# Experts sorted by load: twelve places of 128 slots and twenty of 64, with high and low token parts side by side

## The chip, the core and the metric

The kernel is one launch on one core of a Trainium2 chip. TensorE (PE) multiplies matrices, and its weight loads are a row of their own (PEld); VectorE (DVE), ScalarE (ACT) and GpSimd (POOL) compute elementwise, SyncE (SP) issues most of the DMAs. Each engine takes its own instructions in the order in which they stand. Tensors lie in device memory and pass through SBUF, which has 128 partitions; TensorE adds up in PSUM. The metric is the device time of one execution, in microseconds (us); lower is better.

## The reference

Two transformer blocks on 1024 tokens of width 1024: a mixer with attention and a gated delta rule, then a mixture of experts; a second block with a long convolution (hyena) and a gated feed-forward part. The change lies in the mixture of experts of the first block. Each token picks one of 4 groups and in it 2 of 8 experts, so 2048 pairs of token and gate go to 32 experts:

```python
hid = jax.nn.silu(xblk @ w1[e]) * (xblk @ w3[e])      # w1, w3: 1024 x 512
return hid @ w2[e]                                    # w2: 512 x 1024
...
yb = lax.map(run, (xb, blk_expert)).reshape(cap, D) * buf_w[:, None].astype(t.dtype)
y = jnp.zeros((N, D), t.dtype).at[buf_tok].add(yb)
```

Everything is float32, with sums that are near float32's accuracy.

## The kernel before

**Split products.** TensorE multiplies a shortened format here (fp32r), so every operand is split into hi, its rounding, and lo, the rest. `mm3` (L229 to L233) makes a product of three matmuls: hi(x) hi(w), hi(x) lo(w), lo(x) hi(w). The tokens stand as the stationary operand of 128 columns, one column a slot; the weights move, 512 columns at a time.

**Weights.** Each expert has 6 MB, which come in six pieces of 1 MB: w1 and w3 in two halves each of K (kg), then w2 in two. `weights` (L212 to L227) has SyncE load a piece into raw (L218), ScalarE cast it to hi in two halves of 1024 columns (L223), and VectorE subtract lo = raw - hi in two halves (L226). The pieces of w1 and w3 have four rows of 2 KB in a partition, those of w2 two of 4 KB. There are five raw buffers and three pairs of hi and lo (`wpool "We",5,3`), so a cast waits until TensorE has read the third piece before it, and a load waits for lo of the fifth piece before it.

**A block** (`block` in `moe`) is one expert's work on 128 slots: GpSimd gathers the token rows (L1410, into one of three xg); eight transposes (L1417) put them into PSUM, ScalarE casts xh (L1419), VectorE subtracts xl (L1420); 48 matmuls make h1 and h3 in two PSUM banks (mm); silu on ScalarE (L1432), mul on VectorE (L1433) give hs; four transposes (L1436), sh (L1439), sl (L1440); 24 matmuls with w2 into two banks (acc); VectorE scales by gate and a row (yo, L1455, two of 512 columns); GpSimd adds the rows into d_x in memory (L1456).

**Order of the experts.** `route` counts the tokens of each expert on the chip. The first place is expert 0. Of the others, the three first that have more than 128 tokens get a second gather of 128 slots in their own block (NTWO = 3, at TWO_AT), which shares the pieces. What is over goes to a loop at the end whose count is read from memory (`more`); here it ran no pass. So there are 32 + 3 = 35 gathers and 32 x 6 = 192 pieces.

**Beside it** runs the spectrum: a generator for the filter of the second block, whose matmuls (sp, L327, L354, L362), VectorE operations (L332 to L365) and stores (L367) a scheduler spreads over the blocks. At the end of the routing, val (L1355, L1356) holds for each slot column the token and gate, L1360 multiplies them into columns, and tokI (L1366) is what the gathers read. Behind the stage `hyena` begins with a norm that loads x back (L1501).

Of the kernel before, what the change touches and what calls it, by code (L numbers as in the profile page):

```python
# [8 lines left out]
F32 = mybir.dt.float32  # L9
# [6 lines left out]
P = 128  # L16
S = 1024
D = 1024
EPS = 1e-6
NEXP = 32  # L20
NTWO = 3
TWO_AT = (8, 14, 20)
NBLK = 48
# [6 lines left out]
def shape_constants():  # L30
# [52 lines left out]
    io[:, 156:163] = P * np.arange(1, 8)[None, :]  # L83
# [30 lines left out]
class Builder:  # L114
    def __init__(self, tc, ins, ctx):
        self.tc, self.nc, self.i, self.ctx = tc, tc.nc, ins, ctx
        self.right = 0
        self.cst = ctx.enter_context(tc.tile_pool(name="cst", bufs=1))
# [93 lines left out]
    def weights(self, src, a, b, eng=None, pieces=False):  # L212
# [7 lines left out]
        n = a * b  # L220
# [694 lines left out]
    def attention(self, cx, qn, kn, vv, oaT):  # L915
# [14 lines left out]
        for h in range(4):  # L930
# [84 lines left out]
            self.rsqrt(nrm[5], nrm[3], 65536.0, EPS, "a")  # L1015
# [191 lines left out]
    def route(self, pool, lg):  # L1207

# [94 lines left out]
        V.tensor_sub(ch, two[:, 1:33], two[:, 0:32])
        V.scalar_tensor_tensor(ch1, two[:, 0:32], 1.0, ch, op0=ALU.add, op1=ALU.mult)

        pos, cd = T("pos", 32), T("cd", 32)
        V.tensor_scalar(pos, two[:, 0:32], -1.0, two[:, 32:33], op0=ALU.mult, op1=ALU.add)
        V.tensor_add(pos, pos, io[:, 0:32])
        V.scalar_tensor_tensor(cd, two[:, 0:32], 1.0, pos, op0=ALU.add, op1=ALU.subtract)
        V.tensor_mul(cd, cd, ch)  # L1310
        V.tensor_add(pos, pos, cd)
        V.memset(pos[:, 0:1], 0.0)

        V.tensor_sub(pk, obs[:, 0:32], ch)
        V.tensor_scalar(pk, pk, 1.0, 32.0, op0=ALU.add, op1=ALU.mult)
        V.tensor_add(pk, pk, pos)
        V.scalar_tensor_tensor(pk, ch1, 1024.0, pk, op0=ALU.mult, op1=ALU.add)

        blk, slot = T("blk", 2, 8), T("slot", 2, 8)
        big, q, sel = T("big", 16, 7), T("q", 16), T("sel", 8, 32)  # L1320
        rk, pa = T("rk", 2, 8), T("pa", 2, 8)
        for u in range(2):
            for src, dst in ((R, rk), (pk[:, None, :].to_broadcast([P, 8, 32]), pa)):
                V.tensor_mul(sel, E[u], src)
                V.tensor_reduce(dst[:, u, :], sel, axis=AX.X, op=ALU.add)
        rkf, paf = (x.rearrange("p a b -> p (a b)") for x in (rk, pa))
        blkf, slotf = (x.rearrange("p a b -> p (a b)") for x in (blk, slot))
        V.tensor_tensor(big, rkf[:, :, None].to_broadcast([P, 16, 7]), io[:, None, 156:163].to_broadcast([P, 16, 7]), op=ALU.is_ge)
        V.tensor_reduce(q, big, axis=AX.X, op=ALU.add)
        V.scalar_tensor_tensor(slotf, q, -float(P), rkf, op0=ALU.mult, op1=ALU.add)  # L1330
        pi, ei, oi, ci = (T(n, 16, dt=I32) for n in ("pi", "ei", "oi", "ci"))
        V.tensor_copy(pi, paf)
        V.tensor_scalar(ei, pi, 31, None, op0=ALU.bitwise_and)
        V.tensor_scalar(oi, pi, 5, 31, op0=ALU.logical_shift_right, op1=ALU.bitwise_and)
        V.tensor_scalar(ci, pi, 10, None, op0=ALU.logical_shift_right)

        sec, far, is2 = T("sec", 16), T("far", 16), T("is2", 16)
        V.scalar_tensor_tensor(sec, q, 1.0, ci, op0=ALU.is_equal, op1=ALU.mult)
        V.tensor_scalar(is2, sec, 0.5, None, op0=ALU.is_gt)
        V.scalar_tensor_tensor(far, q, float(NTWO + 30), oi, op0=ALU.add, op1=ALU.add)  # L1340
        V.scalar_tensor_tensor(sec, sec, 31.0, far, op0=ALU.add, op1=ALU.subtract)
        V.tensor_mul(sec, sec, is2)
        V.tensor_add(far, far, sec)
        V.tensor_sub(far, far, ei)
# [530 lines left out]
```

## Time and profile before

| | before |
|---|---|
| median of three runs | 3263.32 us (3260.86 to 3264.44) |
| the profiled execution | 3262.82 us, its span 3261.0 us |
| TensorE matmuls busy | 3098.0 us, 95% |
| TensorE weight loads | 2524.8 us, 77% |
| VectorE | 2440.2 us, 75% |
| ScalarE | 1318.7 us, 40% |
| the experts' stage | from about 1267 to 2000 us |

A busy time is the sum of the durations of an engine's instructions; an engine at 95% can still wait for a few moments in every step. A duration is longer than the step to the next instruction where instructions overlap, so a series is costed by the distance of the starts. The weight-load row shows how long the loading of stationary operands takes, beside the matmuls. In a row of waits the name in front waits for the name behind the arrow.

### The profile page before, as it was taken

To read this page: it belongs to the slowest core of one execution; us is meant where nothing else is said; L and a number is where in the kernel's file an instruction comes from. 1 tells how busy PE (TensorE), PEld (TensorE's weight loads), DVE (VectorE), ACT (ScalarE), POOL (GpSimd) and SP (SyncE) were. 2 spreads that over 40 slices of the span, in tenths; PEclk is the share of its full clock that TensorE was granted. 3 is DMA by queue.
4 is the path that set the end of the run, shared out by engine and by line. 5 is a ranking of instruction groups with operands and counts; after the bars stand their busy time and mean duration, and the time that the engine had idled before them with its cause. 6 is when DMAs were issued, how large, how long until landed. Compare 5 with 4: busy or idle time off the path is not lost.

```text
span 3261.0 us, 42410 instructions
## 1 busy us (share of the span) xinstructions
PE 3098.0 (95%) x15667; PEld 2524.8 (77%) x15667; DVE 2440.2 (75%) x4596; ACT 1318.7 (40%) x2158; POOL 170.8 (5%) x155
## 2 busy tenths in 40 slices
PE   5999999999999977999999997999999999999998
PEld 4778999877777855777777775888878788888886
DVE  7888878757766668887788886777789765755767
ACT  3443333345553214665676664423233221211222
POOL 0001000000000012111121110000000000000000
PEclk9999999999999977999999998999999999999999
DMA  5554332344236544998988996311224221111111
GB/s 193 191 186 129 98 111 87 115 135 144 83 123 231 191 152 150 323 338 276 331 279 273 331 350 208 112 65 65 78 103 172 83 63 44 48 52 52 46 39 71
DMA packets 323789, 499.25 MB, mean 153 GB/s; under 512 B 24586, under 2 KB 179382, under 8 KB 322557
## 3 DMA queue, kind: packets, MB, share of 16 engines
q1 hardware_dynamic: 305693, 465.03, 41.9%
q0 software_dynamic: 10080, 16.81, 2.3%
q10 hardware_dynamic: 7808, 14.68, 1.3%
q8 instruction: 124, 2.03, 0.3%
q14 instruction: 84, 0.69, 0.1%
HBM read 437.95 MB, written 78.41 MB: 158 GB/s over the span
## 4 chain that ended last, share of the span: by engine, by line
PE 54%; DVE 7%; DMA 1%; issue 1%; ACT 1%; DVEq 0%; ACTq 0%; POOLq 0%; SPq 0%
PE mm L239 7%; PE mm L242 7%; PE mm L240 7%; PE mm L231 4%; PE mm L233 3%; PE mm L232 3%; PE acc L233 2%; PE acc L231 2%; PE acc L232 2%; PE sp L362 1%; PE acc L239 1%; PE acc L240 1%; PE acc L242 1%; PE tp L242 1%; PE tp L240 1%; PE tp L239 1%
## 5 line engine op out<-in xcount | busy, mean ns | idle before, releaser
L226 DVE TENSOR_TENSOR lo<-raw,hi 128x1024 fp32r<-128x1024 f32 x464 | 551.1, 1225 | 144.8 <-ACT hi L223 144.3
L223 ACT CAST hi<-raw 128x1024 fp32r<-128x1024 f32 x468 | 471.9, 1049 | 260.6 <-PE acc L233 128.0
L240 PE MATMUL mm<-y_hi,lo 128*128 128x512 f32 x1072 | 419.8, 392 | 0.0
L239 PE MATMUL mm<-y_lo,hi 128*128 128x512 f32 x1072 | 418.9, 391 | 0.0
L242 PE MATMUL mm<-y_hi,hi 128*128 128x512 f32 x1072 | 269.3, 391 | 0.0
L240 PEld LDWEIGHTS mm<-y_hi,lo 128*128 128x128 f32 x1072 | 201.3, 188 | 41.1
L239 PEld LDWEIGHTS mm<-y_lo,hi 128*128 128x128 f32 x1072 | 201.4, 188 | 40.9
L242 PEld LDWEIGHTS mm<-y_hi,hi 128*128 128x128 f32 x1072 | 200.8, 188 | 40.8
L1791 DVE SCALAR_TENSOR_TENSOR cv<-gpad,fcw,cv 128x1024 f32<-128x1024 f32 x176 | 225.9, 1283 | 5.1
L231 PE MATMUL mm<-hi,xh 128*128 128x512 f32 x512 | 202.6, 396 | 0.0
L232 PE MATMUL mm<-lo,xh 128*128 128x512 f32 x512 | 200.7, 392 | 0.2 <-DVE lo L226 0.2
L233 PE MATMUL mm<-hi,xl 128*128 128x512 f32 x512 | 200.7, 393 | 0.0
L239 PE MATMUL mm<-h_lo,hi 128*128 128x512 f32 x448 | 179.1, 400 | 1.0 <-DVE h_lo L210 1.0
L240 PE MATMUL mm<-h_hi,lo 128*128 128x512 f32 x448 | 178.1, 398 | 0.0
L412 DVE SCALAR_TENSOR_TENSOR ada<-araw,c,ada 128x512 f32<-128x512 f32 (+1 forms) x176 | 139.9, 795 | 27.0 <-DMA araw<-in_w_ada 14.2
L239 PE MATMUL mm<-lo,h_hi 128*128 128x256 f32 x512 | 135.5, 295 | 0.1
L240 PE MATMUL mm<-hi,h_lo 128*128 128x256 f32 x512 | 132.8, 290 | 0.0
L242 PE MATMUL mm<-h_hi,hi 128*128 128x512 f32 x448 | 122.8, 400 | 0.0
L231 PEld LDWEIGHTS mm<-hi,xh 128*128 128x128 f32 x512 | 96.5, 189 | 23.4 <-ACT xh L1419 2.3
L233 PEld LDWEIGHTS mm<-hi,xl 128*128 128x128 f32 x512 | 96.6, 189 | 21.5 <-DVE xl L1420 1.3
L1735 ACT CAST hi<-raw 128x2048 fp32r<-128x2048 f32 (+2 forms) x36 | 63.7, 1770 | 119.8 <-PE tp L242 104.1
L232 PEld LDWEIGHTS mm<-lo,xh 128*128 128x128 f32 x512 | 96.6, 189 | 19.9 <-DVE lo L226 0.6
(605 smaller groups left out, 6762.6 us busy)
## 6 DMA issues: line engine op xcount, KB each, us to landing
raw<-in_w SPq DMA_DIRECT2D x192, 1024.0 KB
araw<-in_mod_w SPq DMA_DIRECT2D x96, 256.0 KB
raw<-in_w_in SPq DMA_DIRECT2D x22, 1024.0 KB
raw<-in_ffn_w_up SPq DMA_DIRECT2D x44, 512.0 KB
araw<-in_w_ada SPq DMA_DIRECT2D x64, 256.0 KB
raw<-in_hy_w_in SPq DMA_DIRECT2D x12, 1024.0 KB
araw<-in_w_ada SPq DMA_DIRECT2D x16, 512.0 KB
d_G<-cy ACTq DMA_DIRECT2D x16, 512.0 KB
```

Of the source, the lines that this page charges most:

```text
L223: nc.scalar.copy(fh[:, qs], fr[:, qs])
L226: (eng or nc.vector).tensor_tensor(fl[:, qs], fr[:, qs], fh[:, qs].bitcast(F32), op=ALU.subtract)
L231: nc.tensor.matmul(out, lhs[0], rhs[0], start=start, stop=False)
L232: nc.tensor.matmul(out, lhs[0], rhs[1], start=False, stop=False)
L233: nc.tensor.matmul(out, lhs[1], rhs[0], start=False, stop=stop)
L239: nc.tensor.matmul(out, a[0], b[1], start=start and k == 0, stop=False)
L240: nc.tensor.matmul(out, a[1], b[0], start=False, stop=False)
L242: nc.tensor.matmul(out, a[0], b[0], start=False, stop=stop and k == n - 1)
L362: nc.tensor.matmul(a, fo[:, j, n, :], sd[4 + j][u], start=j == 0, stop=j == 3)
L412: V.scalar_tensor_tensor(acc, raw, c[:, k:k + 1], acc, op0=ALU.mult, op1=ALU.add)
L1735: nc.scalar.copy(hi, raw)
L1791: nc.vector.scalar_tensor_tensor(c3, g[:, di:di + 16, dj:dj + 64], col(k), c3, op0=ALU.mult, op1=ALU.add)
```

## The change

The experts are sorted by load on the chip into places. Twelve places are large (128 slots): expert 0, and the heaviest as found by the counts; places 1 to 3 have 64 slots more in a second gather, for experts with more than 128 tokens. Twenty are small, with 64 slots, and one gather of 128 rows fetches the tokens of two of them. In a small block the stationary operand holds 64 hi and 64 lo columns side by side, so a k tile needs two matmuls (with lo(w), with hi(w)) rather than three; the two halves of the rows in PSUM are added afterwards (L1470 copies rows 64 to 127 down, L1471 adds). w2 keeps three matmuls, with 64 columns as the stationary operand. The second slots of the three large places are made like small blocks. The order is the first place, then eleven large places, each of the first ten followed by a pair of small ones.

w1 and w3 come as two rows of 4 KB in a partition, and the transposes take the token columns with step 2 to match. Cast and lo of a piece are one instruction of 2048 columns each (`whole`). `route` computes two scans together (over 128, over 64) and a third for what is over, has 57 slot columns rather than 48, and copies the lower half of ten columns to the first partitions (tokB, gateB). A scratch name in a norm and the constants' pool change too.

```diff
-NTWO = 3
-TWO_AT = (8, 14, 20)
-NBLK = 48
+NTWO = 3
+NLARGE = 12
+C1 = NLARGE
+C2 = C1 + (NEXP - NLARGE) // 2
+C3 = C2 + NTWO
+NBLK = C3 + 32
...
-        for q in range(2):
-            qs = slice(q * n // 2, (q + 1) * n // 2)
+        m = 1 if whole else 2
+        parts = [slice(q * a * b // m, (q + 1) * a * b // m) for q in range(m)]
+        for qs in parts:
             nc.scalar.copy(fh[:, qs], fr[:, qs])
-        for q in range(2):
-            qs = slice(q * n // 2, (q + 1) * n // 2)
+        for qs in parts:
             (eng or nc.vector).tensor_tensor(fl[:, qs], fr[:, qs], fh[:, qs].bitcast(F32), op=ALU.subtract)
...
+                m = n // 64 if small else 1
+                x = wk.tile([P, 8, m, 2, n // m], F32R, name="x")
+                for kg in range(2):
+                    t = self.tp((P, 4, n))
+                    for q in range(4):
+                        nc.tensor.transpose(t[:, q, :], xg[0:n, bass.ds(kg * 512 + q // 2 * 256 + q % 2, P, step=2)], self.ident[0:n, 0:n])
+                    ks = slice(4 * kg, 4 * kg + 4)
+                    tt = t.rearrange("p q (m n) -> p q m n", m=m)
+                    nc.scalar.copy(x[:, ks, :, 0, :], tt)
+                    nc.vector.tensor_sub(x[:, ks, :, 1, :], tt, x[:, ks, :, 0, :].bitcast(F32))
...
-                        wt = self.weights(w("w3" if u else "w1")[kg * 512:kg * 512 + 512, :].rearrange("(k p) n -> p k n", p=P), 4, 512, eng if kg == 0 else None)
+                        src = w("w3" if u else "w1")[kg * 512:kg * 512 + 512, :].rearrange("(a p b) n -> p a (b n)", p=P, b=2)
+                        wt = [x.rearrange("p a (b n) -> p (a b) n", b=2) for x in self.weights(src, 2, 1024, eng if kg == 0 else None, True)]
...
+                                    xx = x[:, kk].rearrange("p l n -> p (l n)")
+                                    nc.tensor.matmul(h[n][u], xx, wt[1][:, k, :], start=kk == 0, stop=False)
+                                    nc.tensor.matmul(h[n][u], xx, wt[0][:, k, :], start=False, stop=kk == 7)
...
+                        v = wk.tile([P, 512], F32, name="hs", bufs=3)
+                        for o, a in zip((s, v), h[n]):
+                            nc.scalar.copy(o[0:64], a[64:P])
+                            nc.vector.tensor_add(o[0:64], a[0:64], o[0:64])
+                        nc.scalar.activation(s[0:64], s[0:64], AF.Silu)
+                        nc.vector.tensor_mul(s[0:64], s[0:64], v[0:64])
...
+            for n, b in enumerate(rest):
+                block(place(b), large(b))
+                if n < C2 - C1:
+                    small(C1 + n)
```

What stands in a row, in the names of the program: a number behind a name is one buffer's tile, mm and acc are PSUM banks, hi, lo, raw a piece of the weights.

VectorE, before, one plain block from lo of its first w2 piece to yo (ab and sd are the spectrum's, xl the next block's tokens):

```order
L226 TENSOR_TENSOR lo_16325<-raw_16326,hi_16324 128x1024 x2
L341 TENSOR_TENSOR ab_18864<-ab_18864,sd31_18862 128x512
L332 TENSOR_TENSOR sd40_18873<-sp_18871,win_18869 128x512
L1433 TENSOR_TENSOR hs_16310<-hs_16310,mm_16229 128x512
L226 TENSOR_TENSOR lo_16345<-raw_16346,hi_16344 128x1024 x2
L1440 TENSOR_TENSOR sl_16319<-tp_16313,sh_16318 128x512
L1420 TENSOR_TENSOR xl_16383<-tp_16384,xh_16382 128x512
L226 TENSOR_TENSOR lo_16401<-raw_16402,hi_16400 128x1024 x2
L332 TENSOR_TENSOR sd41_18877<-sp_18875,win_18869 128x512
L226 TENSOR_TENSOR lo_16421<-raw_16422,hi_16420 128x1024
L1455 SCALAR_TENSOR_TENSOR yo_16364<-acc_16322,gateS_12691,g2row_12731 128x512
L1455 SCALAR_TENSOR_TENSOR yo_16364<-acc_16323,gateS_12691,g2row_12731 128x512
```

VectorE, after, one small block over the same part; L1471 are the two adds, L1473 the mul, L1480 sl, L1496 yo:

```order
L230 TENSOR_TENSOR lo_17363<-raw_17364,hi_17362 128x2048
L1471 TENSOR_TENSOR hs_17343<-mm_17285,hs_17343 64x512
L1471 TENSOR_TENSOR hs_17344<-mm_17286,hs_17344 64x512
L230 TENSOR_TENSOR lo_17381<-raw_17382,hi_17380 128x2048
L1473 TENSOR_TENSOR hs_17343<-hs_17343,hs_17344 64x512
L230 TENSOR_TENSOR lo_17416<-raw_17417,hi_17415 128x2048
L1480 TENSOR_TENSOR sl_17357<-tp_17351,sh_17356 128x256
L230 TENSOR_TENSOR lo_17430<-raw_17431,hi_17429 128x2048
L1496 SCALAR_TENSOR_TENSOR yo_17398<-acc_17360,gateS_12705,g2row_12749 64x512
L1496 SCALAR_TENSOR_TENSOR yo_17398<-acc_17361,gateS_12705,g2row_12749 64x512
L230 TENSOR_TENSOR lo_17444<-raw_17445,hi_17443 128x2048
```

Two adds and a whole lo now stand between the last w3 piece and mul, and another whole lo between mul and sl.

ScalarE, before, a plain block from the cast of its first w2 piece to sh:

```order
L223 CAST hi_17117<-raw_17119 128x1024 x2
L1432 ACTIVATE hs_17103<-mm_17021 128x512
L223 CAST hi_17137<-raw_17139 128x1024 x2
L223 CAST hi_17193<-raw_17195 128x1024 x2
L1439 CAST sh_17111<-tp_17106 128x512
```

ScalarE, after, a small block over the same part, up to the cast that waits for the first w2 piece's buffer:

```order
L228 CAST hi_17362<-raw_17364 128x2048
L1470 COPY hs_17343<-mm_17285 64x512
L228 CAST hi_17380<-raw_17382 128x2048
L1470 COPY hs_17344<-mm_17286 64x512
L228 CAST hi_17415<-raw_17417 128x2048
L1472 ACTIVATE hs_17343<-hs_17343 64x512
L1479 CAST sh_17356<-tp_17351 128x256
L228 CAST hi_17429<-raw_17431 128x2048
```

Each copy of a half-sum has a whole cast ahead of it, and silu stands behind a third.

TensorE, before, between the last matmuls with w3 and the first with w2:

```order
L232 MATMUL mm_17192<-lo_17254,xh_17175 128x512
L233 MATMUL mm_17192<-hi_17253,xl_17176 128x512
L362 MATMUL sp_18946<-sd60_18903,dftl_18801 128x512
L362 MATMUL sp_18946<-sd70_18918,dftl_18801 128x512
L362 MATMUL sp_18956<-sd40_18873,dftl_18801 128x512
L1436 MATMUL tp_17276<-ident_66,hs_17273 128x128 x4
L1417 MATMUL tp_17347<-ident_66,xg1_12726 128x128 x4
L362 MATMUL sp_18956<-sd50_18888,dftl_18801 128x512
L231 MATMUL acc_17285<-hi_17287,sh_17281 128x512
L232 MATMUL acc_17285<-lo_17288,sh_17281 128x512
L233 MATMUL acc_17285<-hi_17287,sl_17282 128x512
```

TensorE, after, in a small block at the same place:

```order
L1460 MATMUL mm_17286<-hi_17329,x_17261 128x512
L1459 MATMUL mm_17286<-lo_17330,x_17261 128x512
L1460 MATMUL mm_17286<-hi_17329,x_17261 128x512
L1476 MATMUL tp_17351<-ident_66,hs_17343 128x64 x4
L235 MATMUL acc_17360<-hi_17362,sh_17356 64x512
L236 MATMUL acc_17360<-lo_17363,sh_17356 64x512
L235 MATMUL acc_17361<-hi_17362,sh_17356 64x512
L236 MATMUL acc_17361<-lo_17363,sh_17356 64x512
L237 MATMUL acc_17360<-hi_17362,sl_17357 64x512
L237 MATMUL acc_17361<-hi_17362,sl_17357 64x512
```

The spectrum's matmuls that stood around the transposes of hs (sp) are gone from here: after, the last of them stands in the block of the 22nd expert, before, behind the last block. sl is needed by the fifth matmul rather than the third. On VectorE, ahead of val in the routing, 11 of the spectrum's operations (sd, ab, asum) stand before and 20 after.

## Rows read from the trace of the kernel before

**Rows 1.** Busy time per engine on the page: us, share of span, instructions.

```profile
PE 3098.0 (95%) x15667; PEld 2524.8 (77%) x15667; DVE 2440.2 (75%) x4596; ACT 1318.7 (40%) x2158; POOL 170.8 (5%) x155
```

**Rows 2.** Stretches: length, engines' busy us (instructions), TensorE clock, DMA share, GB/s.

```profile
1862.20:1883.60 21.40, 21.40 (x93) 16.18 (x92) 18.68 (x21) 14.64 (x17) 2.64 (x2) 1.00 0.98 348
...
1462.00:1492.60 30.60, 30.60 (x137) 24.58 (x136) 17.47 (x19) 12.52 (x15) 1.45 (x2) 1.00 0.70 241
1492.60:1522.50 29.90, 29.90 (x131) 22.40 (x130) 24.43 (x28) 17.33 (x21) 7.91 (x5) 1.00 0.82 258
1301.00:1990.00 689.00, 685.62 (x2985) 523.60 (x2986) 584.48 (x632) 457.64 (x530) 101.70 (x71) 1.00 0.90 311
```

**Rows 3.** Timeline of TensorE inside w2: start us, length, instruction.

```profile
1868.39 0.39 PE L232 MATMUL acc<-lo,sh 128*128 128x512 f32 x1
1868.62 0.39 PE L233 MATMUL acc<-hi,sl 128*128 128x512 f32 x1
```

**Rows 4.** Line L1436, transposes of hs: ns min/median/max, first and last start.

```profile
L1436 PE MATMUL tp<-ident,hs x140: 270/273/332, 1280.7 to 1993.6; 128*128 128x128 f32 x140
```

**Rows 5.** Timeline of VectorE in that plain block; brackets: idle before, releaser.

```profile
1863.52 0.68 DVE L1433 TENSOR_TENSOR hs<-hs,mm 128x512 f32<-128x512 f32 x1
1864.12 2.35 DVE L226 TENSOR_TENSOR lo<-raw,hi 128x1024 fp32r<-128x1024 f32 x2
...
1870.81 1.23 DVE L226 TENSOR_TENSOR lo<-raw,hi 128x1024 fp32r<-128x1024 f32 x1 [1.95 <-ACT hi L223]
...
1875.01 6.89 DVE L226 TENSOR_TENSOR lo<-raw,hi 128x1024 fp32r<-128x1024 f32 x6
```

**Rows 6.** Timeline of ScalarE in the same block.

```profile
1869.73 2.00 ACT L223 CAST hi<-raw 128x1024 fp32r<-128x1024 f32 x2 [2.42 <-PE acc L233]
```

**Rows 7.** Groups of the stage, 1250 to 2050: busy us, mean ns, idle before.

```profile
L1455 DVE SCALAR_TENSOR_TENSOR yo<-acc,gateS,g2row 128x512 f32<-128x512 f32 x64 | 45.1, 744 | 7.4 <-PE acc L233 7.4
...
L1410 POOL DMA_INDIRECT xg<-d_h,tokI x35 | 38.0, 1085 | 373.6 <-PE tp L1417 363.5 <-DMA raw<-in_w 9.0 <-issue 0.9
```

**Rows 8.** Groups of a later stage (2450 to 3230) with whole 2048-column pieces.

```profile
L1735 ACT CAST hi<-raw 128x2048 fp32r<-128x2048 f32 x28 | 53.6, 1914 | 113.5 <-PE tp L242 104.1 <-DMA raw<-in_ffn_w_up 9.1 <-PE acc L242 0.2
...
L210 DVE TENSOR_TENSOR lo<-raw,hi 128x2048 fp32r<-128x2048 f32 x28 | 64.0, 2287 | 11.8 <-ACT hi L1735 11.6
```

**Rows 9.** Groups of other stages with 64 partitions or 256 columns.

```profile
L955 ACT CAST kT<-tp 64x512 fp32r<-64x512 f32 x16 | 9.3, 583 | 0.3
...
L956 DVE CAST kT<-tp 64x512 fp32r<-64x512 f32 x16 | 10.7, 682 | 6.7 <-ACT kT L955 6.6
...
L849 DVE TENSOR_TENSOR gXt<-gXt,acc 128x256 f32<-128x256 f32 x96 | 39.9, 418 | 15.2 <-PE acc L792 14.0
```

**Rows 10.** Waits, 1250 to 2020: total us, times, longest.

```profile
ACT hi L223 <- PE acc L233: 128.0, 59, 5.3
...
ACT hi L223 <- DMA raw<-in_w: 3.4, 3, 1.8
...
SPq L218 <- DVE lo L226: 537.5, 183, 9.0
```

**Rows 11.** Four stretches around an idle time of TensorE, in an earlier stage.

```profile
1018.00:1021.40 3.40, 3.40 (x16) 2.63 (x14) 1.82 (x2) 1.05 (x1) 0.00 (x0) 1.00 1.00 315
1021.40:1024.60 3.20, 0.18 (x2) 0.03 (x1) 1.96 (x3) 2.09 (x2) 0.00 (x0) 1.00 1.04 379
1024.60:1028.00 3.40, 3.40 (x8) 2.45 (x9) 2.40 (x2) 1.04 (x1) 0.00 (x0) 0.52 0.86 273
1028.00:1032.00 4.00, 3.41 (x15) 2.43 (x15) 1.22 (x1) 1.05 (x1) 0.00 (x0) 0.98 0.87 343
```

**Rows 12.** Timelines of TensorE and VectorE at the end of routing.

```profile
1244.20 6.58 PE L1360 MATMUL acc<-r_val,r_ls 128*128 128x96 f32 x32 [0.66 <-DVE r_val L1356]
...
1251.77 3.07 DVE L1366 CAST tokI<-r_row 128x48 int32<-128x48 f32 x1
```

**Rows 13.** Timeline of ScalarE behind the stage.

```profile
2014.40 1.04 ACT L223 CAST hi<-raw 128x1024 fp32r<-128x1024 f32 x1 [19.00 <-DMA d_spec<-so]
```

More of the change, by code (lines that the diff above doesn't have):

```diff
@@ L210, in lo, with weights @@
         self.nc.vector.tensor_sub(out, src, hi.bitcast(F32))
-    def weights(self, src, a, b, eng=None, pieces=False):
+    def weights(self, src, a, b, eng=None, whole=False):
         nc = self.nc
@@ L1322, in route @@
-        for u in range(2):
[L1323 to L1344, printed above, removed]
-        V.scalar_tensor_tensor(far, q, 0.5, far, op0=ALU.is_gt, op1=ALU.mult)
@@ L1346, in route @@
-        V.tensor_add(blkf, far, ei)
+        for k, lim in ((0, 128.0), (1, 64.0)):
+            V.tensor_scalar(ob[0][:, k, 2:33], cnt[:, 1:32], lim, None, op0=ALU.is_gt)
+        run = sums(ob)
+        s2, s1, n2, n1 = run[:, 0, 0:32], run[:, 1, 0:32], run[:, 0, 32:33], run[:, 1, 32:33]
+        pos, p1, d1, d2 = T("pos", 32), T("p1", 32), T("d1", 32), T("d2", 32)
+        V.tensor_scalar(pos, s1, -1.0, n1, op0=ALU.mult, op1=ALU.add)
+        V.tensor_add(pos, pos, io[:, 0:32])
+        V.tensor_sub(p1, s1, s2)
@@ new lines, in route @@
+        V.tensor_scalar(p1, p1, n2, 1.0, op0=ALU.add, op1=ALU.add)
+        V.tensor_sub(d1, p1, pos)
+        V.scalar_tensor_tensor(d1, cnt, 64.0, d1, op0=ALU.is_gt, op1=ALU.mult)
+        V.scalar_tensor_tensor(d2, s2, 1.0, p1, op0=ALU.add, op1=ALU.subtract)
+        V.scalar_tensor_tensor(d2, cnt, 128.0, d2, op0=ALU.is_gt, op1=ALU.mult)
+        V.tensor_add(pos, pos, d1)
+        V.tensor_add(pos, pos, d2)
+        V.memset(pos[:, 0:1], 0.0)
+        cap, two, beg, mov, far = (T(n, 32) for n in ("cap", "two", "beg", "mov", "far"))
@@ new lines, in route @@
+        V.tensor_reduce(nb, gtm, axis=AX.X, op=ALU.add)
+        oc = [T("oc0", 1, 33), T("oc1", 1, 33)]
+        for x in oc:
+            V.memset(x, 0.0)
+        V.tensor_copy(oc[0][:, 0, 1:33], nb)
+        obs = sums(oc)[:, 0]
+        V.tensor_scalar(beg, pos, float(NLARGE), None, op0=ALU.min)
+        V.tensor_add(beg, beg, pos)
+        V.tensor_scalar(beg, beg, 64.0, None, op0=ALU.mult)
+        V.tensor_scalar(mov, two, 2.0 * (C2 - 2), None, op0=ALU.mult)
+        V.scalar_tensor_tensor(far, obs[:, 0:32], 128.0, beg, op0=ALU.mult, op1=ALU.subtract)
@@ L1441, in block @@
                     hs.append((sh, sl))
[L1442 removed]
+                y = [[(self.mm if n < len(slots) - 1 else self.acc)() for _ in range(2)] for n in N]
                 for kg in range(2):
[L1444 to L1445 removed]
+                    wt = self.weights(w("w2")[kg * 256:kg * 256 + 256, :].rearrange("(k p) n -> p k n", p=P), 2, 1024, None, True)
+                    for n, (sh, sl) in zip(N, hs):
+                        rows = slots[n][0]
                         for k in range(2):
@@ L1470, in moe, with place, large @@
-            for b in order:
-                reg = nc.sync.value_load(self.order[0:1, b - 1:b], min_val=0, max_val=31)
-                block(of(reg), [col(b)] + ([col(31 + b)] if b <= NTWO else []))
+            def place(b):
+                return of(nc.sync.value_load(self.order[0:1, b - 1:b], min_val=0, max_val=31))
+            def large(b):
+                tg = lambda c, n: (self.tokI[0:n, c:c + 1], self.gateS[0:n, c:c + 1])
+                t, g = tg(b, P)
+                slots = [(P, gather(t), t, g)]
+                if 0 < b <= NTWO:
+                    t, g = tg(C2 + b - 1, 64)
+                    slots.append((64, gather(t, 64, True)[:, :, 0], t, g))
+                return slots
@@ new lines, in small @@
+            def small(c):
+                x = gather(self.tokI[:, c:c + 1], P, True)
+                for e, (t, g) in enumerate(((self.tokI[0:64, c:c + 1], self.gateS[0:64, c:c + 1]),
+                                            (self.tokB[:, c - C1:c - C1 + 1], self.gateB[:, c - C1:c - C1 + 1]))):
+                    block(place(NLARGE + 2 * (c - C1) + e), [(64, x[:, :, e], t, g)])
+            block(lambda nm: I[nm][0, 0], large(0), nc.gpsimd)
+            rest = list(range(NTWO + 1, NLARGE))
```

163 lines of the change are left out of this document (81 added, 82 removed).

## The prediction

> **What bounds the kernel now.** I read the page first: TensorE shows 95% of the span busy [rows 1], so the question is whether that holds in the stage that changes. The table of stretches answers it [rows 2]. One plain block, 1862.2 to 1883.6, takes 21.40 us, and TensorE is busy for all of it, VectorE for 18.68, ScalarE for 14.64. A block with a second gather takes 30.60 + 29.90 = 60.5 us with the plain block behind it, so the second slots cost 39.1 - 21.4 = 17.7 us; DMA is at 0.70 there and VectorE at 17.47 of 30.6: that one is bound by TensorE. From 1301 to 1990 TensorE is busy 685.6 of 689 us at the full clock. The transposes of hs start at 1280.7 and 1993.6 first and last [rows 4]: 31 intervals in 713 us, close to 31 x 21.4 + 3 x 17.7 = 716.5.
>
> So TensorE ends last, but the others stand close behind. VectorE has 2.7 us of slack in a plain block, no more. The waits [rows 10] show a ring: ScalarE's hi cast waits 128.0 us in 59 waits for the second matmuls (acc), because only three hi/lo buffers exist; VectorE's lo waits for that cast; SyncE waits 537.5 us for lo to give raw back. The casts waited for their DMA only 3.4 us in all, three times, so transfers end first. What must be asked of a shorter TensorE part is how far the ring VectorE, cast, buffer lets it through.
>
> **TensorE's work falls.** One 512-column matmul follows the other by 0.23 us [rows 3]. Before, each of the 35 gathers has 48 + 24 = 72 of them, some 16.5 us, and 12 transposes, about 1 us (one is 0.27 [rows 4], overlapping the next): 17.6, with the spectrum's matmuls filling up to 21.4. After, 12 large blocks keep that; 20 small blocks and three second parts have 32 + 24 = 56, or 13.4 us. That is 23 x 4.2 = 97 us less TensorE work. It is the most that this edit can bring.
>
> **VectorE's work does not fall.** A weight piece of 2048 columns costs it one subtraction rather than two: 2.29 us alone [rows 8], 2.20 back to back if it overlaps its neighbour as a 512-wide one does (0.68, but 0.60 to the next [rows 5]); before, 6.89 for six halves, 2.30 a piece [rows 5]. Six pieces: 13.2, against 13.8. A small block adds two additions of 64x512 for the halves; 64 partitions are no cheaper than 128 (0.682 [rows 9]), so 1.2. Mul is 0.6, sl 0.36 (0.418 [rows 9]), the two yo 1.33 (0.744 each [rows 7], less the overlap). Per small block 13.2 + 1.2 + 0.6 + 0.36 + 1.33 = 16.7 us, plus half of a shared xl. So even a perfect small block is no shorter than about 17 us.
>
> **The small block, step by step.** VectorE's new order is lo(w2a), two adds, lo(w2b), mul, lo(next w1a), sl, lo(next w3a), two yo, and two more lo. Call 0 the end of lo for the last w3 piece. Its 8 matmuls end at about 2.0. VectorE does lo(w2a) to 2.2; ScalarE copies the second half-sum 2.1 to 2.7 (0.583 [rows 9]); the adds end at 3.4; lo(w2b) at 5.6; silu on ScalarE stands behind a cast of 1.914 [rows 8] and is done by 5.2; mul ends at 6.2. Before, the last matmul led to silu and mul at once; now a copy, an add and a whole 2.2 us lo lie between, and TensorE has nothing from 2.0 to 6.2. Then come transposes to about 7.0, the sh cast to 7.5 (shorter than that copy), and four matmuls to 8.4. VectorE meanwhile does lo(next w1a) to 8.4 and sl to 8.8; only then do the other eight w2a matmuls run, to 10.7. The next w3a piece needs the hi/lo buffer that w2a holds, so its cast runs 10.75 to 12.7 and lo starts there: a hole of about 4 us on VectorE. Before, the same place had a hole of 1.95, with half casts of 1 us (2.00 for two) [rows 5, 6]; the whole cast lengthens it. The sum is 16.8 + 4.0 = 20.85 us against 21.4. **The small block is then no longer bound by TensorE, and it gains half a microsecond, not four.** Bounds: 17 with no hole, 22.5 where spectrum work stands in the queue.
>
> **Large blocks.** After a small pair comes a large block. Its xl (two at 0.6) stands on VectorE behind the yo, at 16.3 to 17.5 on the clock above, and its third product waits for it; from there its four pieces need 4 x 12 x 0.227 = 10.9 us of TensorE. From last w3 matmul to last w3 matmul that is 24.4 to 25.3, say 24.9. From large to first small it is 20 to 21.8, say 20.5, as the large block's own chain has silu and mul without copies. A triple is 24.9 + 20.5 + 20.85 = 66.25, against 3 x 21.4 = 64.3. Ten triples: **+19.5** (by the ends of the legs +9 to +41; lower only if the hole closes, which is R1).
>
> **Second slots.** Three of them, at 56 matmuls and 0.7 us of transposes rather than 72: 12.5 us rather than 17.7, as TensorE bounds there. **-15.6** (0 to -17).
>
> **Spectrum work on VectorE** (0.6 us an operation [rows 5]) was covered by the 2.7 us of slack. In small blocks there is none outside the hole. In the order, five small blocks carry two or three such operations outside it, 13 in all: **+8** (0 to +15).
>
> **Clock.** Where TensorE had run 0.18 us in a stretch of 3.20, the stretch of 3.40 us after it was granted 0.52, the lower level of 1.2 GHz, and ran 8 matmuls where 16 ran in 3.40 us before [rows 11]. A small block has TensorE waiting about 4.2 us before its transposes. Eight matmuls at the low level cost 3.4 - 8 x 0.227 = 1.6 us more; part falls while sl is awaited. I take 0.8 for each of 20: **+16** (0 to +35). The Trainium skill ("TensorE: Matmul & The Clock Gate", HAM oscillation — how this bites in real kernels) says that kernels with few rows that wait between groups of matmuls fall to the low clock every time and lose by it. It agrees with the row; its rule is R2 below.
>
> **Routing.** Two scans rather than one, about 3.5 us of small operations on a VectorE that was nearly full; 20 rather than 11 spectrum operations now stand ahead of val, 9 x 0.6 = 5.4; L1360's 32 matmuls of 96 columns (6.58 us [rows 12]) get 114, some 0.5. Part of that lies beside the transfers of the first weights, and the work that moved ahead leaves the first block 2 us shorter. tokI, at 1251.77 [rows 12], comes later by **+7** (0 to +11).
>
> **Tail.** TensorE's spectrum work now ends with ten experts to go; before it went on behind the last block and a hi cast waited 19.00 us for the spectrum's store, until 2014.40 [rows 13]. The loads of x need the scatter (SyncE waited 11.4 us for it), which stays: **-3** (0 to -8).
>
> **4 KB rows** are a DMA matter. The ring gives raw back too late for DMA to matter [rows 10], so nothing, unless the interval falls below about 18 us. The step-2 transposes, the renamed scratch and the constants' pool: nothing.
>
> **Sum.** 19.5 - 15.6 + 8 + 16 + 7 - 3 = +31.9 us. The profiled execution took 3262.82, half a microsecond under the median of 3263.32, so about 3295.
>
> **Rivals.** *R1, faster.* The relief gets through: VectorE's hole closes, as casts and w2a matmuls slip under other work. TensorE at 100% in every stretch [rows 2] speaks for it; VectorE's 17 us floor and the three buffers speak against. If small blocks came at 17 to 18, 20 x 3.7 = 74 us go, with the second slots 90, less 7 for routing: 3262.8 - 90 + 7 - 3 = 3177. Halfway, at 19.5 us and large blocks at 22, 20 x 1.9 - 10 x 0.6 + 15.6 - 4 gives about 3219. The other terms leave 8 + 16 + 7 - 3 - 15.6 = 12.4 us to be earned by ten triples, so it decides at a triple of 63.1 us: small blocks at 20.5 with 22 for the large leg, or 19.5 with 24. The Trainium skill ("Perfetto Trace Analysis", Identifying the Most-Contended Engine) holds that busy matmuls overstate TensorE and its weight loads should be read instead. By that rule TensorE has slack already, 16.18 of 21.40 being 76%, and taking work off it is worth less; it speaks against R1 and this change.
>
> *R2, slower still.* The low clock lasts on: in each small block all 24 w2 matmuls and the next piece's run at 0.43 rather than 0.23 us (1.6 us for every eight). With 2 to 3 us more on the path in 20 blocks, 40 to 60: 3335 to 3355. Against it, the row after the low one is back at 0.98 [rows 11].
>
> *R3, the change does not do what it says.* If more than eleven of experts 1 to 31 carry over 64 tokens, or over three carry more than 128, the closing loop runs; every pass is a serial block of at least 21 us. Before, the 35 gathers [rows 7] are 32 + 3, so nothing overflowed there, but the new capacities are other ones; two overflows give 3340.
>
> **How the numbers follow.** Forecast 0.58, its own range 3265 to 3325; R1 0.27; R2 0.12; R3 0.03. A measurement of this kernel tells 0.2%, about 6.5 us, from no change. Slower: 0.47 of the forecast + 0.15 of R2 and R3 = 0.62. Same: 0.08 + 0.04 of R1 = 0.12. Faster: 0.03 + 0.23 = 0.26. The range reaches down into half of R1 and up to the start of R2: 3205 to 3330.
>
> **What would show it.** Right: transposes of hs 20 to 22 us apart in small pairs, 24 to 25 before a large block; ScalarE's hi cast waiting for acc in every small block, and a VectorE gap of about 4 us behind sl; TensorE clearly under full in the stage, with stretches granted less than 1.00; VectorE above 80%. Wrong: small intervals under 19 us (R1), or clock under 0.8 over the stage (R2), or more than 35 large and small gathers (R3: 12 + 10 + 3 = 25 are due). tokI more than 11 us later, or not at all later, would make the routing term wrong.

## The result, and the profile after

The changed kernel takes 3361.31 us in the median (3357.9 to 3365.47) against 3263.78: 1.030 times as long, interval 1.028 to 1.032. The forecast was slower, and slower it is, but by 97 us and not by 32; the time lies above the range. The profiled execution has a span of 3356.1 us, 95.1 more than before.

The page's busy shares, to be read beside [rows 1]:

```profile
PE 3077.4 (92%) x15219; PEld 2438.3 (73%) x15219; DVE 2438.7 (73%) x4447; ACT 1305.6 (39%) x1990; POOL 237.0 (7%) x143
```

The transposes of hs, to be read beside [rows 4]:

```profile
L1476 PE MATMUL tp<-ident,hs x140: 216/273/472, 1286.7 to 2075.8; 64*128 64x64 f32 x92, 128*128 128x128 f32 x48
```

This row cuts the 95 us into three. The first transposes start 6.0 us later than the 1280.7 of [rows 4]; the 31 intervals take 789.1 us and not 712.9, which is 76.2; and what lies behind the last block takes 12.9 us longer (3356.1 - 2075.8 = 1280.3, before 1267.4), though none of its code changed.

A late small block, one without spectrum work, on VectorE (start, length, instruction, idle before and releaser):

```profile
1966.83 6.68 DVE L230 TENSOR_TENSOR lo<-raw,hi 128x2048 fp32r<-128x2048 f32 x3
1973.43 1.48 DVE L1471 TENSOR_TENSOR hs<-mm,hs 64x512 f32<-64x512 f32 x2
1974.83 2.27 DVE L230 TENSOR_TENSOR lo<-raw,hi 128x2048 fp32r<-128x2048 f32 x1
1977.03 0.68 DVE L1473 TENSOR_TENSOR hs<-hs 64x512 f32<-64x512 f32 x1
1977.63 2.28 DVE L230 TENSOR_TENSOR lo<-raw,hi 128x2048 fp32r<-128x2048 f32 x1
1979.84 0.41 DVE L1480 TENSOR_TENSOR sl<-tp,sh 128x256 fp32r<-128x256 f32 x1
1985.02 2.29 DVE L230 TENSOR_TENSOR lo<-raw,hi 128x2048 fp32r<-128x2048 f32 x1 [4.78 <-ACT hi L228]
```

and on TensorE:

```profile
1973.10 0.40 PE L1460 MATMUL mm<-hi,x 128*128 128x512 f32 x1
1977.77 0.64 PE L1476 MATMUL tp<-ident,hs 64*128 64x64 f32 x4 [4.27 <-DVE hs L1473]
```

and in stretches (length, busy us of TensorE, weight loads, VectorE, ScalarE and GpSimd, granted clock, DMA share, GB/s), the second just behind that wait and the third the whole block:

```profile
1977.80:1981.40 3.60, 3.60 (x13) 2.41 (x14) 2.45 (x2) 0.37 (x1) 0.00 (x0) 0.53 1.04 336
1966.30:1989.00 22.70, 15.04 (x62) 9.84 (x61) 17.80 (x14) 13.77 (x12) 7.71 (x2) 0.92 0.82 291
```

This is the block of the prediction: adds, a whole lo, mul, a whole lo, sl, then a hole. TensorE waits 4.27 us for mul where 4.2 was said, and runs at a granted 0.53 behind it. It came out at 22.7 us, not at 20.85 and 0.8: the hole behind sl is 4.78 us rather than 4, and VectorE is busy for 17.80 us of the stretch rather than 16.8. But such blocks are the good ones. The scheduler puts other work into others, and in four of the 23 small parts (20 blocks and three second parts) it puts two whole lo between the second add and mul; there TensorE waits 5.9 to 6.7 us. One of the four:

```profile
1587.20 4.47 DVE L230 TENSOR_TENSOR lo<-raw,hi 128x2048 fp32r<-128x2048 f32 x2
1591.60 0.68 DVE L1473 TENSOR_TENSOR hs<-hs 64x512 f32<-64x512 f32 x1
```

### The profile page after: what moved, and what is told of

Read it like the earlier page. It is cut to its first block, busy times and chain, and to the rows that moved or that the text cites. A ratio compares the mean times of both kernels' runs of the same rounds, so it can differ in the third digit from the quotient of the medians.

```text
span 3356.1 us, 41235 instructions
## 1 busy us (share of the span) xinstructions
PE 3077.4 (92%) x15219; PEld 2438.3 (73%) x15219; DVE 2438.7 (73%) x4447; ACT 1305.6 (39%) x1990; POOL 237.0 (7%) x143
## 5 line engine op out<-in xcount | busy, mean ns | idle before, releaser
L230 DVE TENSOR_TENSOR lo<-raw,hi 128x2048 fp32r<-128x2048 f32 (+1 forms) x274 | 531.7, 1957 | 220.0 <-ACT hi L228 216.7
L228 ACT CAST hi<-raw 128x2048 fp32r<-128x2048 f32 (+1 forms) x276 | 449.6, 1644 | 270.3 <-PE acc L237 144.5
L1459 PE MATMUL mm<-lo,x 128*128 128x512 f32 x320 | 137.5, 430 | 26.7 <-DVE lo L230 22.3
L1460 PE MATMUL mm<-hi,x 128*128 128x512 f32 x320 | 128.0, 400 | 0.0
L1497 POOL DMA_INDIRECT d_x<-yo,tokI x25 | 96.5, 3859 | 345.4 <-DVE yo L1496 311.5
L235 PE MATMUL acc<-hi,sh 128*64 128x512 f32 (+1 forms) x256 | 117.2, 458 | 3.5 <-ACT sh L1479 3.5
L236 PE MATMUL acc<-lo,sh 128*64 128x512 f32 (+1 forms) x256 | 111.4, 435 | 0.0
L1848 DVE TENSOR_SCALAR cv<-gpad,fcw,fcb 128x1024 f32<-128x1024 f32 x22 | 17.9, 814 | 121.7 <-ACT gpad L1842 121.6
```

What stands on the lines that cost most here:

```text
L235: nc.tensor.matmul(out, lhs[0], rhs[0], start=start, stop=False)
L236: nc.tensor.matmul(out, lhs[0], rhs[1], start=False, stop=False)
L1459: nc.tensor.matmul(h[n][u], xx, wt[1][:, k, :], start=kk == 0, stop=False)
L1460: nc.tensor.matmul(h[n][u], xx, wt[0][:, k, :], start=False, stop=kk == 7)
L1497: nc.gpsimd.indirect_dma_start(out=self.x1, out_offset=bass.IndirectOffsetOnAxis(ap=tcol, axis=0), in_=yo[0:rows], in_offset=None, bounds_ ...
```

## The experiments

**Where is the loss behind the stage?** The feed-forward part has the same code in both kernels and TensorE is busy for all of it at the full clock. A stretch of 100 us there, of before and of after:

```profile
2740.00:2840.00 100.00, 100.00 (x443) 82.79 (x442) 69.67 (x54) 25.18 (x28) 0.00 (x0) 1.00 0.17 53
```

```profile
2825.60:2925.60 100.00, 100.00 (x437) 81.69 (x436) 66.39 (x51) 24.59 (x27) 0.00 (x0) 1.00 0.14 43
```

Fewer matmuls in the same time (443 against 437), with nothing idle. In the built programs every fp32r tile on the left side of SBUF starts at a multiple of 256 bytes before the change, and 128 bytes off after it. The cause is the one line that makes the constants' pool by `self.pool`: it pads the pool's size to 256 bytes, but the pool itself begins at address 16512, which is 128 past a multiple. Before, its size brought the end to 18432, a multiple. One kernel undoes that alone (called the aligned kernel below):

```diff
         self.cst = ctx.enter_context(self.pool("cst"))
+        self.cst.rest = 128
```

> The changed kernel with one line more: the constants' pool is padded so that what lies above it in SBUF starts at a multiple of 256 bytes, as it did before the change (in the changed kernel all left-hand tiles start 128 bytes off). Theory A (operands that start 128 bytes off slow the matmuls): the step between matmuls in the feed-forward part goes back from 0.230 to 0.227 us, the part behind the experts gives back some 14 us and the experts' stage some 10, so about 3335 us. Rival (this chip or this program runs TensorE slower for another reason): 3361, step still 0.230.

Measured: 3346.17 us, 1.0248 of before (1.0231 to 1.0265), so 15 us less than the changed kernel. The other does it to the kernel before:

```diff
         self.cst = ctx.enter_context(tc.tile_pool(name="cst", bufs=1))
+        self.cst.tile([P, 32], F32, name="pad")
```

> The kernel before with 128 unused bytes added to the constants' pool, nothing else. Theory A: the same loss without any of the change: matmul step 0.230 in the feed-forward part and 0.232 in the experts' stage, 20 to 30 us, so 3284 to 3294 us. Rival: 3264, unchanged.

Measured: 3292.39 us, 1.0084 (1.0067 to 1.0101): 29 us from 128 bytes that nothing uses. The same stretch, first of the aligned changed kernel, then of the kernel before with the pad:

```profile
2825.60:2925.60 100.00, 100.00 (x443) 82.81 (x442) 69.28 (x54) 25.66 (x28) 0.00 (x0) 1.00 0.17 53
```

```profile
2770.00:2870.00 100.00, 100.00 (x437) 81.95 (x437) 70.02 (x56) 24.78 (x28) 0.00 (x0) 1.00 0.17 53
```

443 matmuls with the tiles at multiples of 256 bytes, 437 without. Theory A holds; in the changed kernel it gives back 15 and not 25. That TensorE no longer bounds the experts' stage there would explain the rest; no run tests that.

**Is it the low clock?** Matmuls of no use fill TensorE's wait for mul; a second kernel has two of them instead of five.

```diff
+                        dd = self.tp((P, 512))
+                        for q in range(5):
+                            nc.tensor.matmul(dd, self.ident[0:64, :], v[0:64], start=True, stop=True)
                         nc.vector.tensor_mul(s[0:64], s[0:64], v[0:64])
```

> The aligned changed kernel, with five matmuls of no use (the identity times the second half-sum, into a spare PSUM bank) between the adds and the transposes of hs in each small block and second part, so that TensorE has work while it waits for mul. Theory B (the low clock behind the idle time costs about 2 us on the path of each small block): granted clock of the stage back above 0.98 and 25 to 40 us less than the aligned kernel. Rival (the chain of copy, add, lo, mul and the buffers sets the interval whatever the clock): the same time as the aligned kernel within 5 us, or a little more.

> As the kernel with matmuls of no use in the gap, with two of them rather than five, since five ran 4.56 us and held up the transposes of hs. Theory B (the low clock behind the gap costs some 2 us in each small block): 10 to 25 us less than the aligned kernel's 3346. Rival: no gain, 3340 to 3360 us, as the interval is set by VectorE, ScalarE and the buffers.

Measured: 3378.01 us with five (1.0343, 1.0325 to 1.036) and 3341.34 with two (1.0236, 1.0219 to 1.0253), against the aligned 3346.17. In a block of the first (the five stand as ten instructions in the row):

```profile
2063.55 4.56 PE L1476 MATMUL tp<-hs,ident 64*128 64x512 f32 x10 [1.54 <-DVE hs L1472]
2067.95 0.40 PE L1480 MATMUL tp<-ident,hs 64*128 64x64 f32 x4
```

The four transposes take 0.40 us there, not 0.64: the clock had stayed up, but the fillers held the transposes back. Five cost 32 us, two gain 5, with the runs of both kernels overlapping (3335.0 to 3346.1, 3341.9 to 3348.7). With two, the clock fell all the same. Just behind that wait in a late block:

```profile
2043.00:2047.00 4.00, 3.18 (x13) 2.43 (x13) 3.88 (x5) 0.96 (x2) 0.00 (x0) 0.57 1.00 314
```

And over the stage, from the first transposes of hs to the last, in the aligned kernel, with five fillers, with two, and in the aligned kernel with halves that comes below:

```profile
1290.80:2075.10 784.30, 674.64 (x2643) 456.18 (x2641) 603.25 (x498) 459.86 (x386) 177.82 (x62) 0.93 0.82 282
1291.80:2115.40 823.60, 784.26 (x2874) 500.94 (x2872) 605.74 (x498) 461.06 (x386) 193.42 (x62) 0.93 0.78 269
1285.30:2066.10 780.80, 720.30 (x2735) 472.93 (x2733) 604.90 (x498) 460.32 (x386) 195.02 (x62) 0.93 0.82 283
1287.60:1993.00 705.40, 650.17 (x2627) 446.36 (x2625) 611.35 (x678) 472.69 (x569) 180.42 (x62) 0.95 0.89 311
```

Above 0.98 was expected of the fillers, and 0.93 it stayed. So they do not decide theory B. An estimate from these rows bounds it: at 0.93 the stage loses at most 0.07 x 784, some 55 us, of TensorE's full-clock time, with halves 0.05 x 705, some 35. Of the 82 us between the aligned kernel and the one with halves (below) the clock alone can then make up about 20 at most.

**Is it the small block at all?** All 32 places large, the rest of the change kept:

```diff
-NLARGE = 12
+NLARGE = 32
...
-            for n, at in enumerate((2, 5, 8)):
+            for n, at in enumerate((8, 14, 20)):
```

> The aligned changed kernel with all 32 places large: no small blocks, but whole casts, 4 KB rows, the new routing and the 64-slot second parts stay. Theory C (the small blocks with their longer chain cost the time): interval back near 21.4 us, second parts some 4 us cheaper each, routing 6 us dearer, so 3255 to 3275 us. Rival (whole 2048-column casts and subtractions cost it, in large blocks too): intervals of 22.5 us and more, 3300 us or more.

Measured: 3313.62 us, 1.0144 (1.0123 to 1.0166). The rival won: without one small block, 50 us are still lost. Two stretches, one with spectrum work on TensorE and one late without:

```profile
1327.00:1438.00 111.00, 111.00 (x472) 83.47 (x471) 93.46 (x73) 68.62 (x53) 16.53 (x11) 1.00 0.99 352
1940.00:2040.00 100.00, 88.33 (x357) 71.15 (x356) 72.93 (x51) 57.05 (x43) 8.66 (x6) 0.86 0.74 264
```

The first holds five blocks of 22.2 us; in the second, TensorE has gaps and a low clock, and blocks take 23.9. What is left in common with the changed kernel, beside the longer routing and the 4 KB rows, is the whole pieces. So these were taken back in two kernels:

```diff
-        m = 1 if whole else 2
+        m = 2
```

> The aligned changed kernel with cast and lo of each weight piece in two halves of 1024 columns, as before the change; small blocks, 4 KB rows and routing stay. Theory D (whole pieces lengthen the chain between the last w3 matmul and the next cast, in every block): 30 to 45 us less than the aligned kernel's 3346, so 3300 to 3316 us, small-to-small intervals near 22 us. Rival C (the small block's copies and adds are what costs): 3335 to 3346 us.

> The kernel with all 32 places large, with halves rather than whole pieces. Theory D: intervals back at 21.4 us, so about 3262 us: 3264, less some 13 for the 64-slot second parts, plus 10 to 12 for the longer routing. Rival (4 KB rows or the new routing cost it): 3290 us or more.

and put alone into the kernel before, `m = 1` for the experts' pieces and nothing else:

> The kernel before with one edit: cast and lo of each expert weight piece as one 2048-column instruction. Theory D: intervals of 22 us and more where the spectrum fills TensorE's gaps and near 23.9 without it, 30 to 45 us, so 3294 to 3309 us. Rival (whole pieces cost nothing in a kernel that TensorE bounds): 3264 us.

Measured: 3264.38 us with small blocks and halves (0.9994, 0.9984 to 1.0004); 3261.41 with large places only and halves (0.9984, 0.9975 to 0.9994); 3304.86 for the kernel before with whole pieces (1.0125, 1.0108 to 1.0142). Whole pieces cost 82 us of the aligned kernel's 83, 52 with large places only, and 39 in the kernel before. So whole pieces are what costs; theory D was about twice too small for the small blocks, and its mechanism, a longer chain in every block, is not seen in all of them. The spectrum's own instructions (behind the length stands what they keep TensorE busy, and their count), in five early and four late blocks, first with all places large and whole pieces, then with halves:

```profile
1337.80:1448.10 110.30, 22.59 (x49) 8.66 (x48) 7.84 (x12) 1.21 (x3) 1.00 0.99 352
1926.00:2021.50 95.50, 0.00 (x0) 0.00 (x0) 0.00 (x0) 0.00 (x0) 0.86 0.78 276
```

```profile
1310.90:1418.20 107.30, 18.80 (x41) 7.24 (x40) 6.57 (x10) 0.58 (x1) 1.00 0.99 348
1907.00:1992.80 85.80, 15.05 (x33) 5.79 (x32) 5.88 (x9) 1.17 (x2) 1.00 0.86 304
```

With whole pieces the scheduler packs the spectrum more tightly into the early blocks: 3.8 us more of it in five, which are 3.0 us longer, with TensorE full in both. It then runs out, and the late blocks, with nothing of it to do, take 23.9 us where those with halves take 21.4 and do 3.8 us of it each. The early blocks are longer by what is packed into them; the late ones are a loss. How much of the whole is the chain and how much the spectrum's place, no run separates, since none holds that place fixed. A late small block with halves:

```profile
1966.73 2.34 DVE L231 TENSOR_TENSOR lo<-raw,hi 128x1024 fp32r<-128x1024 f32 x2
1969.02 0.68 DVE L1472 TENSOR_TENSOR hs<-mm,hs 64x512 f32<-64x512 f32 x1
1969.63 1.21 DVE L231 TENSOR_TENSOR lo<-raw,hi 128x1024 fp32r<-128x1024 f32 x1
1970.76 0.68 DVE L1474 TENSOR_TENSOR hs<-hs 64x512 f32<-64x512 f32 x1
1971.36 2.35 DVE L231 TENSOR_TENSOR lo<-raw,hi 128x1024 fp32r<-128x1024 f32 x2
1973.64 0.42 DVE L1481 TENSOR_TENSOR sl<-tp,sh 128x256 fp32r<-128x256 f32 x1
...
1975.53 1.22 DVE L231 TENSOR_TENSOR lo<-raw,hi 128x1024 fp32r<-128x1024 f32 x1
1979.57 1.23 DVE L231 TENSOR_TENSOR lo<-raw,hi 128x1024 fp32r<-128x1024 f32 x1 [2.83 <-ACT hi L229]
```

Only half a lo stands between the second add and mul, a half of the next piece goes into the hole, and what is left of it is 2.83 us where it was 4.78. From its transposes of hs to the next ones 20.4 us pass. What TensorE waits for, by name, from 1300 to 2000 (total us, times, longest), in the aligned kernel and then with halves:

```profile
PE tp L1477 <- DVE hs L1474: 47.9, 13, 6.6
PEld tp L1477 <- DVE hs L1474: 42.1, 11, 7.0
PEld mm L1460 <- DVE lo L231: 32.1, 34, 6.4
```

```profile
PE tp L1477 <- DVE hs L1474: 34.9, 12, 5.3
PEld tp L1477 <- DVE hs L1474: 21.4, 7, 5.7
PEld mm L1460 <- DVE lo L231: 5.4, 14, 0.8
```

Both the waits for mul and those for a piece's lo are shorter.

**Cast or subtraction?** Only one of the two whole, aligned, in two kernels (casts in `cut(1)` and lo in `cut(2)`, and the other way):

```diff
+        cut = lambda m: [slice(q * a * b // m, (q + 1) * a * b // m) for q in range(m)]
-        for qs in parts:
+        for qs in cut(1 if whole else 2):
             nc.scalar.copy(fh[:, qs], fr[:, qs])
-        for qs in parts:
+        for qs in cut(2):
```

> The aligned changed kernel with the cast of a piece whole (2048 columns) and lo in halves. Theory E1 (the whole cast is what costs: the next piece's cast starts only when TensorE has let the buffer go, and VectorE waits for all of it): 3320 to 3346 us, near the aligned kernel's 3346. Theory E2 (the whole subtraction costs, as mul and sl stand behind it): 3270 to 3290 us. If both share: 3300 to 3315 us.

> The aligned changed kernel with the cast in halves and lo whole. Theory E1: 3270 to 3290 us. Theory E2: 3320 to 3346 us. If both share: 3300 to 3315 us.

Measured: 3288.20 us with the whole cast (1.0084, 1.0063 to 1.0106), 3342.20 with the whole lo (1.0239, 1.0221 to 1.0257). The subtraction alone costs 78 us, the cast alone 24, both together 82: theory E2, though the two do not add up. Then lo whole in some pieces only (`whole` false for the w2 pieces, or for those of w1 and w3):

> The aligned changed kernel with casts in halves everywhere and lo whole only in the pieces of w1 and w3 (in halves for w2). Theory H1 (a whole lo costs where TensorE waits for the piece itself, since its matmuls start 1.1 us later): most of the 78 us between 3264 and 3342 stay, as four of six pieces are whole: 3310 to 3330 us. Theory H2 (it costs where mul and sl stand behind it): mul stands behind lo of a w2 piece, sl behind lo of a w1 piece, so about half stays: 3295 to 3310 us.

> The same with lo whole only in the two w2 pieces. Theory H1: 3280 to 3295 us. Theory H2: 3300 to 3315 us.

Measured: 3291.05 us (1.009, 1.0066 to 1.0113) with w1 and w3 whole, 3289.56 (1.0072, 1.0055 to 1.0089) with w2 whole. Neither theory fits both (the second time lies in the range of H1, the first in neither): four whole pieces cost 27 us and two cost 25, and the two together are less than the 78 of all six. A whole lo of w2 costs twice as much a piece as one of w1 or w3, which speaks for mul behind it, but the sum is missing 26 us. Why is not shown; the scheduler's order differs in each of these kernels.

**What bounds the small blocks with halves?** Two kernels, from the aligned one with halves: four pairs of hi and lo and three raw buffers, and lo of the first w2 piece on GpSimd in small blocks.

```diff
-            self.wpool(cx, "We", 5, 3, side="right")
+            self.wpool(cx, "We", 3, 4, side="right")
```

> The aligned changed kernel in halves, with four pairs of hi and lo and three raw buffers rather than three and five. Theory F (with three pairs the next piece's cast must wait for w2 matmuls of this block, the hole on VectorE): small intervals of 18 to 19 us, 3225 to 3245 us. Rival (VectorE's own work and the chain set the interval, or three raw buffers make the casts wait for DMA): 3260 us or more.

```diff
-                    wt = self.weights(w("w2")[kg * 256:kg * 256 + 256, :].rearrange("(k p) n -> p k n", p=P), 2, 1024, None, True)
+                    wt = self.weights(w("w2")[kg * 256:kg * 256 + 256, :].rearrange("(k p) n -> p k n", p=P), 2, 1024, nc.gpsimd if kg == 0 and slots[0][0] < P else None, True)
```

> The aligned changed kernel in halves, with lo of the first w2 piece on GpSimd in the small blocks (2.4 us a half there, 1.15 on VectorE). Theory G (VectorE bounds the small blocks): 2.3 us less VectorE work in each, up to 40 us less, 3225 to 3250 us. Rival (the slower GpSimd stands in the chain ahead of w2, or its scatter and gather queue up behind it): 3264 us or more.

Measured: 3300.67 us (1.0117, 1.0078 to 1.0156) and 3357.28 (1.0291, 1.0272 to 1.031). Both times are in the rivals' ranges. The waits of the first (total us, times, longest), over the stage:

```profile
ACT hi L229 <- DMA raw<-in_w: 144.3, 89, 5.1
...
ACT hi L229 <- PE acc L238: 27.3, 13, 4.7
```

The wait for the buffer is nearly gone (27.3 us, 128.0 in the kernel before [rows 10]), but a new one for the transfer takes its place (144.3, there 3.4): three raw buffers let too little be loaded ahead. In the second, VectorE and GpSimd subtract at the same time:

```profile
2013.07 7.22 POOL L231 TENSOR_TENSOR lo<-raw,hi 128x1024 fp32r<-128x1024 f32 x2 [1.99 <-issue]
```

```profile
2015.47 5.91 DVE L231 TENSOR_TENSOR lo<-raw,hi 128x1024 fp32r<-128x1024 f32 x2
```

Two halves take VectorE 5.91 us here and 2.35 in the block with halves above. Moving work off VectorE slowed VectorE.

## Why the prediction was wrong, point by point

- **TensorE's relief does not come through: right, and more so than was said.** Three kernels by the transposes of hs, first and last start (712.9 us in the kernel before): aligned with halves, the same with all places large, and the kernel before with the pad:

```profile
L1477 PE MATMUL tp<-ident,hs x140: 221/272/366, 1287.6 to 1993.4; 64*128 64x64 f32 x92, 128*128 128x128 f32 x48
L1473 PE MATMUL tp<-ident,hs x140: 222/273/329, 1289.6 to 1993.1; 128*128 128x128 f32 x128, 64*128 64x64 f32 x12
L1437 PE MATMUL tp<-ident,hs x140: 271/273/329, 1285.7 to 2007.4; 128*128 128x128 f32 x140
```

  With small blocks the stage takes 705.8 us, 7 less than before; without one small block it takes 703.5. So what arrives comes by the shorter second parts, and the small blocks bring nothing. Yet TensorE did bound the kernel before: the pad slows its matmuls by 1.4% (437 for 443), and the stage becomes 721.7 us. The Trainium skill ("Perfetto Trace Analysis", Identifying the Most-Contended Engine) has TensorE's headroom judged by its weight loads and its share of peak arithmetic, not by busy matmuls. By the weight loads it had slack, 16.18 us of 21.40 in [rows 2]; this measurement says otherwise. What stopped the relief was VectorE and the chain close behind. VectorE's work for a small block was said to be 16.7 us; in the aligned kernel the stretch of a late one shows 16.71 in 22.0:

```profile
2026.10:2048.10 22.00, 15.77 (x62) 10.08 (x61) 16.71 (x13) 13.07 (x10) 7.62 (x1) 0.89 0.84 313
```

- **The step that failed first: "the constants' pool: nothing".** It costs 15 us in this kernel and 29 in the kernel before, and was put at nothing without a reason. Nothing in a trace of before could show it; the addresses of the built program could. Without it the time would still be above the range, at 3346.
- **The step that failed most: the legs of the triple.** One late block's order was worked out and taken for all. With the aligned kernel, small to small took 24.2 us on average over ten legs (20.85 and 0.8 for the clock were said, with 0.8 for the spectrum), large to small 23.7 (20.5), small to large 22.6 (24.9). A triple is 70.4 us, not 66.25 and its share of the clock. Whole pieces were costed as a gain of 0.1 us each on VectorE and as a longer hole in small blocks; they are what costs 82 us here and 39 in the kernel before. With halves, small to small takes 21.0 us on average, large to small 20.8 and small to large 21.5. That a whole lo keeps TensorE from starting on the first half of a piece, and shuts mul and sl out for 2.2 us where they could slip in after 1.1, was not charged anywhere outside the one block; the waits above show both kinds. Nor was it charged that the scheduler then finishes the spectrum early and leaves the late blocks without it. How the 82 us divide among these stays open.
- **Second slots, -15.6: wrong in this kernel, and mis-added.** By the prediction's own prices, 16 matmuls fewer at 0.227 and 0.3 us of transposes take some 4 us off 17.7, not 5.2, so about -12. A two-slot leg with the next takes 64.7 us in the aligned kernel, 18.5 more than two plain legs, so no gain over the 17.7 of [rows 2]. With all places large and halves, where TensorE bounds, the three take 57.2, 55.2 and 58.0 us (60.5, 60.8 and 60.3 before), 11.2 less in all.
- **Clock, +16: open.** The low level behind the wait for mul is there, at 0.53, where it was said to be. The Trainium skill ("TensorE: Matmul & The Clock Gate", HAM oscillation — how this bites in real kernels) has the low clock come back every time in a kernel with few rows that waits between its groups of matmuls; the trace agrees at this wait (0.53 behind 4.27 us of waiting). What it costs no run shows: two fillers did not keep the clock up, and with five the transposes came later.
- **Spectrum work on VectorE, +8.** No run takes this term apart from the legs.
- **Signs.** The clock was to be below 1.00 in stretches, the hole behind sl about 4 us: both came. Legs of 20 to 22 us in small pairs and 24 to 25 before a large block did not (24.2 and 22.6). VectorE was to be above 80%, and is busy for 603.25 of 784.3 us in the aligned kernel, 77%: it waits more rather than works more.
- **Routing, +7: near.** tokI comes 10.9 us later, the upper bound that was given, and the first transposes of hs 6.0.

```profile
1262.63 2.15 DVE L1380 CAST tokI<-r_row 128x57 int32<-128x57 f32 x1
```

- **Tail, -3: right in size.** From the last yo to the transposes of the norm 29.4 us pass (2083.48 to 2112.91), 31.5 before. Of the 12.9 us lost behind the stage, the aligned kernel has 9.2 back.
- **4 KB rows: nothing, as far as the runs show.** Large places with halves and 4 KB rows stand at 3261.
- **Rivals.** R1 was the wrong side. R2 came nearest in size (3335 to 3355), but its sign, a clock under 0.8 over the stage, did not show: 0.93 was granted. R3 did not happen: 25 gathers, as were due.

## What to carry to other kernels

Merging two instructions into one saves a fixed part of 0.1 us here and takes away the place between them: ask what else on that engine, and which consumer of the first half, used it, and what a scheduler does with the room. An edit to a pool is an edit to every address above it, so compare the addresses of the built programs before costing it at nothing. And where an engine's relief is 97 us on paper, look first how far the next engine stands behind: 2.7 us a block was all that could pass, and the stage shows nothing of it even with halves.

The best of the versions keeps all places large with 64-slot second parts, halves and aligned pools, at 3261.41 us, 0.9984 of before (0.9975 to 0.9994).

## What the runs showed of the hardware

- fp32r tiles that start 128 bytes past a multiple of 256 slow TensorE with no idle time and no lower clock in the records: 437 matmuls of 512 columns in 100 us, not 443.
- With GpSimd subtracting in SBUF, VectorE's 1024-column subtraction takes 2.95 us each in one place (5.91 for two), where 1.15 is usual; over that kernel's stage the mean is 1.437 us, with halves alone 1.220. GpSimd's own took 3.13 on average, where 2.40 was measured in the first block of the kernel before.

```profile
L231 POOL TENSOR_TENSOR lo<-raw,hi 128x1024 fp32r<-128x1024 f32 x40 | 118.0, 3131 | 12.9 <-issue 9.3 <-ACT hi L229 3.5
...
L231 DVE TENSOR_TENSOR lo<-raw,hi 128x1024 fp32r<-128x1024 f32 x328 | 460.3, 1437 | 111.8 <-ACT hi L229 111.6
```

- 64 partitions cost VectorE and ScalarE as much as 128, as [rows 9] had it: in the changed kernel L1471 and L1470 on 64x512 took 0.678 and 0.580 us, L1439 and L1438 on 128x512 0.679 and 0.582.
